# Whole-tile instructions for the middle tiles of a SiLU-and-multiply kernel

## The chip, the cores and the metric

The kernel runs on one core of one Trainium2 chip; the metric is device time in microseconds (us). "Span" in a profile is the time from its first to its last instruction, about 2 us less than the device time of the same run. ACT is the engine that evaluates functions (ScalarE), DVE the one that works on vectors (VectorE), SP the one that here issues stores (SyncE). Sixteen DMA engines move data between HBM and the on-chip memory. MB are 10^6 bytes; the profile's "4096.0 KB" is 4096 x 1024 bytes.

## The reference, cut to what matters

```python
x = np.random.randn(32, 512, 2048).astype(np.float32)   # 16384 rows of 2048

def reference(x):
    x1, x2 = x[..., :1024], x[..., 1024:]
    return (x1 * (1 / (1 + np.exp(-x1))) * x2).astype(np.float32)
```

134.22 MB are read and 67.11 MB written, each once. The arithmetic is one activation over half of the input and one multiply of the two halves.

## The kernel before

The rows are cut into 16 tiles. A tile has 128 partitions with K = 8 rows each: 8.39 MB in, 4.19 MB out. Input and output each have two buffers. Loads are issued from ACT's instruction stream, stores from SP's.

```python
K = 8
KC = 2
in_pool = ctx.enter_context(tc.tile_pool(name="in_pool", bufs=2))
out_pool = ctx.enter_context(tc.tile_pool(name="out_pool", bufs=2))
# ... load(i): nc.scalar.dma_start(out=xt..., in_=view(x_flat, i)) ...
load(0)
load(1)
for i in range(n_tiles):
    # ...
    for c in range(0, k, KC):               # 4 chunks of 2 rows
        ce = min(c + KC, k)
        nc.scalar.activation(out=ot[:, c:ce, :], in_=xt[:, c:ce, :half], func=Silu)   # shortened
        nc.vector.tensor_mul(out=ot[:, c:ce, :], in0=ot[:, c:ce, :], in1=xt[:, c:ce, half:])
        if last:
            nc.sync.dma_start(out=ov[:, c:ce, :], in_=ot[:, c:ce, :])
    if not last:
        nc.sync.dma_start(out=ov, in_=ot[:, :k, :])
    if i + 2 < n_tiles:
        load(i + 2)                          # waits for the tile's last multiply
```

With four chunks, DVE multiplies chunk 0 while ACT works on chunk 1: in the timeline below, ACT works from 73.53 to 80.84 us and DVE from 75.47. The schedule is kept as written: each engine does its instructions in this order, as when the next load's issue at 84.40 us follows the last multiply's end at 84.37.

## Time and profile before

| | before |
|---|---|
| device time | 470.82 us (470.62 to 471.04, 3 runs) |
| ACT busy, DVE busy | 25%, 30% of the span |
| DMA | 201.35 MB, 429 GB/s over the span |
| from one tile's start to the next | 29.03 us (mean of 14; the prediction takes 29.06) |

First, the totals by engine from the page of the kernel before: busy us, share of the span, instructions.

```profile
DVE 142.3 (30%) x64; ACT 118.2 (25%) x65; POOL 0.2 (0%) x4
```

Both compute engines are idle for more than two thirds of the time. The window table shows who is not. Its columns are the stretch and its length, busy us (and instructions) of DVE, ACT and POOL, the granted clock, the mean busy share of the DMA engines, and GB/s.

```profile
44.50:55.40 10.90, 8.89 (x4) 7.31 (x4) 0.00 (x0) 1.00 1.00 433
55.40:73.50 18.10, 0.00 (x0) 0.00 (x0) 0.00 (x0) 1.00 1.00 434
...
102.60:200.00 97.40, 35.20 (x16) 29.23 (x16) 0.00 (x0) 1.00 1.01 436
```

The DMA share is 1.00 whether the compute engines work (first line) or idle (second). The kernel is bound by DMA. Next, the timeline of two middle tiles: start, length, engine, source line, operation, and in brackets the idle time before it and what ended it.

```profile
73.53 7.31 ACT L87 ACTIVATE ot<-xt 128x2048 f32<-128x2048 f32 x4 [21.68 <-DMA xt<-in_x_dram]
75.47 8.90 DVE L92 TENSOR_TENSOR ot<-ot,xt 128x2048 f32<-128x2048 f32 x4 [20.09 <-ACT ot L87]
84.40 0.37 ACTq L74 DMA_DIRECT2D xt<-in_x_dram  x1
102.62 7.31 ACT L87 ACTIVATE ot<-xt 128x2048 f32<-128x2048 f32 x4 [21.78 <-DMA xt<-in_x_dram]
```

A tile starts at 73.53 and the next at about 102.6. Compute takes 10.9 us, then both engines wait 18 us more for data. Last, the chain of waits that ended last (start, length, what), and the DMA issues with the median time from issue to landing.

```profile
55.41 47.19 DMA xt<-in_x_dram
...
102.62 1.92 ACT ot L87
...
104.57 8.91 DVE ot L92 x4
```

```profile
out_dram<-ot SPq DMA_DIRECT2D x15, 4096.0 KB, 39.8
xt<-in_x_dram ACTq DMA_DIRECT2D x16, 47.1
```

The tiles arrive every 29 us, so a load waits 18 us of its 47 behind the load before it (issued at 55.41 us, with the load before it landing at about 73.5).

### The profile page before, as it was taken

To read this page: it belongs to the slowest core of one execution; us is meant where nothing else is said; L and a number is where in the kernel's file an instruction comes from. 1 tells how busy PE (TensorE), PEld (TensorE's weight loads), DVE (VectorE), ACT (ScalarE), POOL (GpSimd) and SP (SyncE) were. 2 spreads that over 40 slices of the span, in tenths; PEclk is the share of its full clock that TensorE was granted. 3 is DMA by queue.
4 is the path that set the end of the run, shared out by engine and by line. 5 is a ranking of instruction groups with operands and counts; after the bars stand their busy time and mean duration, and the time that the engine had idled before them with its cause. 6 is when DMAs were issued, how large, how long until landed. Compare 5 with 4: busy or idle time off the path is not lost.

```text
span 468.9 us, 269 instructions
## 1 busy us (share of the span) xinstructions
DVE 142.3 (30%) x64; ACT 118.2 (25%) x65; POOL 0.2 (0%) x4
## 2 busy tenths in 40 slices
DVE  0070705106061160601507025070250702407034
ACT  1142406023060330603206032060420604106051
POOL 0000000000000000000000000000000000000000
DMA  9899999999999998999999999999999989999998
GB/s 431 375 447 403 447 447 447 403 419 431 447 447 403 447 492 363 442 492 391 458 403 439 456 447 403 409 442 447 447 403 444 467 386 447 442 419 481 400 409 354
DMA packets 5042, 201.35 MB, mean 429 GB/s; under 512 B 560, under 2 KB 560, under 8 KB 560
## 3 DMA queue, kind: packets, MB, share of 16 engines
q10 hardware_dynamic: 2304, 134.22, 66.4%
q1 hardware_dynamic: 2736, 67.11, 33.2%
q14 instruction: 2, 0.02, 0.0%
HBM read 134.22 MB, written 67.11 MB: 429 GB/s over the span
## 4 chain that ended last, share of the span: by engine, by line
DMA 80%; DVE 15%; ACT 3%; DVEq 0%; issue 0%
DMA xt<-in_x_dram 80%; DVE ot L92 15%; ACT ot L87 3%; DVEq L128 0%
## 5 line engine op out<-in xcount | busy, mean ns | idle before, releaser
L92 DVE TENSOR_TENSOR ot<-ot,xt 128x2048 f32<-128x2048 f32 x64 | 142.3, 2286 | 319.5 <-ACT ot L87 319.5
L87 ACT ACTIVATE ot<-xt 128x2048 f32<-128x2048 f32 x64 | 116.9, 1897 | 338.8 <-DMA xt<-in_x_dram 338.8
L87 ACT ACT_TABLE_LOAD x1 | 1.3, 1283 | 1.3 <-PEq L117 1.3
L117 POOL MEMSET const-uint8-127<- 128x1 uint8 x1 | 0.1, 102 | 0.0
L117 POOL MEMSET const-bfloat16-1.0<- 128x1 bf16 x1 | 0.1, 101 | 0.0
L117 POOL MEMSET const-float32-0.0<- 128x1 f32 x1 | 0.1, 98 | 0.2 <-issue 0.2
L117 POOL MEMSET const-float32-1.0<- 128x1 f32 x1 | 0.1, 98 | 0.0
## 6 DMA issues: line engine op xcount, KB each, us to landing
out_dram<-ot SPq DMA_DIRECT2D x15, 4096.0 KB, 39.8
out_dram<-ot SPq DMA_DIRECT2D x4, 1024.0 KB, 5.7
xt<-in_x_dram ACTq DMA_DIRECT2D x16, 47.1
```

Source lines behind the costliest of these rows:

```text
L87: nc.scalar.activation(out=ot[:, c:ce, :], in_=xt[:, c:ce, :half], func=mybir.ActivationFunctionType.Silu,)
L92: nc.vector.tensor_mul(out=ot[:, c:ce, :], in0=ot[:, c:ce, :], in1=xt[:, c:ce, half:],)
L117: nc = _bacc.Bacc("TRN2", target_bir_lowering=False, num_devices=1)
```

## The change

The intent is fewer, longer instructions. Tiles 1 to 14 take one activation and one multiply over all 8 rows, without the overhead of three further instructions on each engine. The first tile keeps its chunks so that the pipeline starts early, the last so that its stores can start early. The price is that within a middle tile DVE can no longer start before ACT has done the whole tile.

```diff
-    KC = 2
+    KC_EDGE = 2
...
-        for c in range(0, k, KC):
-            ce = min(c + KC, k)
+        kc = KC_EDGE if i in (0, n_tiles - 1) else k
+        for c in range(0, k, kc):
+            ce = c + kc
```

## The prediction

> **What bounds the kernel now.** The DMA engines. The page's slices show DMA at 9 tenths nearly throughout; the window table gives a DMA share of about 1.00 and 431 to 436 GB/s in every stretch from 44.5 to 451 us. 201.35 MB at 433 GB/s is 465 us of the 468.9 us span. DVE is busy for 30%, ACT for 25%. [...]
>
> The chain of waits alternates a load of 47.1 us, one ACT op of 1.92 us and four DVE ops of 8.91 us, for every second tile. But 47.1 us is no transfer time: tiles start 29.06 us apart (73.5 and 102.6 in the timeline), so 18 us of it is queueing behind the previous load. Each tile has 8 load packets of 64 KB and 8 store packets of 32 KB per DMA engine (from the page's queue counts); taken in turn, 96 KB at 433/16 GB/s is 3.63 us, and eight rounds are 29.05 us: the measured period.
>
> **What the change does to compute.** On tiles 1 to 14, ACT and DVE no longer overlap. One ACT op is 1893 ns, four take 7.31 us. [...] One DVE op takes 2284 ns, four take 8.90 us; 8192 elements should take about 8.7 us (estimate). Load end to last multiply grows from 10.87 us to about 15.75 us, so store i and load i+2 are issued 4.9 us later; the first at about 60.3 us instead of 55.4. Saved are three op overheads per tile and engine, worthless on engines idle two thirds of the time. Bytes, packets, first and last tile stay.
>
> **How much is on the critical path.** Read literally, the chain says seven changed tiles times 4.9 us: 34 us slower. I expect none of it. Load i+2 comes 15.75 us after load i landed, while load i+1 keeps the load queue filled until 29.06 us: 13 us of slack. Store i-1 lands 21.7 us after load i (11.0 + 39.8 - 29.06), so the store queue is still filled when store i comes, with some 6 us left. Tile i's activation needs store i-2 landed, 7.4 us before load i. If the store queue ran dry for a packet, loads would take the turn and bytes only change order. The tail is the same tile in the same chunks.
>
> **Predicted:** 470.8 us, 8 times in 10 between 469.6 and 472.2. Faster by over 2%: 0.01; within 2%: 0.96; slower by over 2%: 0.03.
>
> **What the profile should show.** ACT ops of 7.0 and DVE ops of 8.7 us on the middle tiles; ACT busy about 114.6 us, DVE about 140; tile starts still 29.06 us apart, the last at 451.0; issue to landing of loads down from 47.1 to about 42.2 us, of stores from 39.8 to about 34.9; the chain's DMA share down from 80% to about 72%, ACT up from 3% to 11%; DMA share still 1.00.
>
> **What would make it wrong.** [...] If store buffers come free too late, ACT would wait for a store. If an 8192-element op over eight strided rows cost more per element, the 13 us would shrink.

The forecast of 470.8 us is the time before, with none of the chain's 34 us added. The 34 us are seven times 4.9, and the sum behind the 4.9 us came to 15.75 us from load end to last multiply, against 10.87: about 7.0 us for the activation, 8.7 us for the multiply, and small gaps. The activation's term measured 7.03 us. The 8.7 us is the estimate beside the 8.90 us of four chunks; it measured 8.69 us.

## The result, and the profile after

| | before | after |
|---|---|---|
| device time, same rounds (6 runs each) | 470.94 us | 470.88 us |
| range | 470.62 to 471.61 | 470.64 to 471.60 |
| load landed to last multiply done, middle tile | 10.9 us | 15.8 us |
| load, issue to landing | 47.1 us | 42.2 us |
| store, issue to landing | 39.8 us | 34.8 us |

The ratio is 1.0 with a 95% interval of 0.9987 to 1.0013. Here and below, ratios are the mean time of one kernel's fast runs over that of the other's of the same rounds, so not quite the ratio of the quoted medians. The profiled run of the changed kernel was its slowest (471.6 us, span 469.5 us); that of before took 470.65 us. The 0.6 us between the spans is within the runs' scatter and says nothing about the change.

The totals by engine after:

```profile
DVE 139.5 (30%) x22; ACT 114.3 (24%) x23; POOL 0.2 (0%) x4
```

The groups of instructions by shape after (line, engine, operation, shapes, count, busy us, mean ns, idle before):

```profile
L93 DVE TENSOR_TENSOR ot<-ot,xt 128x8192 f32<-128x8192 f32 x14 | 121.7, 8692 | 283.8 <-ACT ot L88 283.8
L88 ACT ACTIVATE ot<-xt 128x8192 f32<-128x8192 f32 x14 | 98.4, 7029 | 301.9 <-DMA xt<-in_x_dram 301.9
```

ACT saved 3.9 us and DVE 2.8 us of busy time, on engines that were waiting anyway. The windows after:

```profile
44.50:60.30 15.80, 7.97 (x1) 7.03 (x1) 0.00 (x0) 1.00 1.07 462
60.30:73.50 13.20, 0.72 (x1) 0.00 (x0) 0.00 (x0) 1.00 0.92 400
...
102.60:200.00 97.40, 28.74 (x4) 28.12 (x4) 0.00 (x0) 1.00 1.00 434
```

A packet is counted where it starts, so short windows scatter (the first two); the long one shows a share of 1.00 and 434 GB/s, as before. The timeline after:

```profile
74.18 7.03 ACT L88 ACTIVATE ot<-xt 128x8192 f32<-128x8192 f32 x1 [21.89 <-DMA xt<-in_x_dram]
81.24 8.69 DVE L93 TENSOR_TENSOR ot<-ot,xt 128x8192 f32<-128x8192 f32 x1 [20.23 <-ACT ot L88]
89.97 0.37 ACTq L74 DMA_DIRECT2D xt<-in_x_dram  x1
103.21 7.03 ACT L88 ACTIVATE ot<-xt 128x8192 f32<-128x8192 f32 x1 [22.00 <-DMA xt<-in_x_dram]
```

The next load is issued 15.8 us after the tile's start instead of 10.9, and the next tile still starts 29.03 us after this one. The chain and the issues after:

```profile
61.05 42.13 DMA xt<-in_x_dram
...
103.21 7.04 ACT ot L88
...
110.27 8.70 DVE ot L93
```

```profile
out_dram<-ot SPq DMA_DIRECT2D x15, 4096.0 KB, 34.8
xt<-in_x_dram ACTq DMA_DIRECT2D x16, 42.2
```

Compute on the chain grew by 4.9 us per pair of tiles, and the load's time from issue to landing shrank by as much. The load did not get faster: it was queued later, behind the same work.

### The profile page after: what moved, and what is told of

Same layout as the page of the kernel before. It is cut to its first block, busy times and chain, and to the rows that moved or that the text cites. A ratio compares the mean times of both kernels' runs of the same rounds, so it can differ in the third digit from the quotient of the medians.

```text
span 469.5 us, 185 instructions
## 1 busy us (share of the span) xinstructions
DVE 139.5 (30%) x22; ACT 114.3 (24%) x23; POOL 0.2 (0%) x4
## 4 chain that ended last, share of the span: by engine, by line
DMA 72%; DVE 14%; ACT 11%; DVEq 0%; issue 0%
DMA xt<-in_x_dram 72%; DVE ot L93 14%; ACT ot L88 11%; DVEq L129 0%
## 5 line engine op out<-in xcount | busy, mean ns | idle before, releaser
L93 DVE TENSOR_TENSOR ot<-ot,xt 128x8192 f32<-128x8192 f32 (+1 forms) x22 | 139.5, 6362 | 322.9 <-ACT ot L88 322.9
L88 ACT ACTIVATE ot<-xt 128x8192 f32<-128x8192 f32 (+1 forms) x22 | 113.0, 5163 | 343.3 <-DMA xt<-in_x_dram 343.3
## 6 DMA issues: line engine op xcount, KB each, us to landing
out_dram<-ot SPq DMA_DIRECT2D x15, 4096.0 KB, 34.8
xt<-in_x_dram ACTq DMA_DIRECT2D x16, 42.2
```

## The experiments

All twelve runs gave correct results. Two theories of why the time stood still, and rivals:

- **Slack.** The DMA queues hold enough work that later issues are absorbed. The cost is zero until the queues run dry, and shows in full where nothing is queued.
- **Cancelling.** The saved overhead repays the lost overlap.
- **Utilisation.** Longer compute costs nothing as long as no engine comes near 100% busy.

### serial_chunks: lose the overlap, save no instruction

Middle tiles do four activations, then four multiplies:

```diff
+        if not edge:
+            for c in range(0, k, KC):
+                nc.scalar.activation(out=ot[:, c:c + KC, :], ...)
+        for c in range(0, k, KC) if edge else range(k - KC, -1, -KC):
             ...tensor_mul of chunk c...
```

> The kernel before with, on tiles 1 to 14, all four activations of 2 rows first and then the four multiplies (in reverse order, so that the first waits for the last activation): the overlap is lost, no op is saved. Load end to last multiply about 16.2 us (7.31 + 8.90) against 10.87. Theory of slack (the DMA queues hold work for some 13 us of loads and 6 us of stores more): same, 470.9 us within 0.3%. Rival, two effects that cancel (fewer op overheads gain what the lost overlap costs): here only the loss is left, so slower; at most 14 x 5.3 = 74 us, clearly over 2%.

Measured: 470.83 us (5 runs) against 470.86 us, ratio 1.0001 (0.9989 to 1.0014). The timeline shows that the edit did what it should: the multiplies start only when the fourth activation is done, and the next tile still starts 29.1 us after this one.

```profile
73.97 7.31 ACT L88 ACTIVATE ot<-xt 128x2048 f32<-128x2048 f32 x4 [21.53 <-DMA xt<-in_x_dram]
81.31 8.90 DVE L101 TENSOR_TENSOR ot<-ot,xt 128x2048 f32<-128x2048 f32 x4 [19.94 <-ACT ot L88]
...
103.05 7.31 ACT L88 ACTIVATE ot<-xt 128x2048 f32<-128x2048 f32 x4 [21.77 <-DMA xt<-in_x_dram]
```

The loss of overlap alone, with no saving beside it, costs nothing. The cancelling theory falls.

### one_buf_chunks and one_buf_whole: take the slack away

Both kernels with one input buffer; nothing is queued behind a load.

```diff
-    in_pool = ctx.enter_context(tc.tile_pool(name="in_pool", bufs=2))
+    in_pool = ctx.enter_context(tc.tile_pool(name="in_pool", bufs=1))
...
-    load(1)
...
-        if i + 2 < n_tiles:
-            load(i + 2)
+        if i + 1 < n_tiles:
+            load(i + 1)
```

> The kernel before with one input buffer instead of two: load i+1 is issued after the last multiply of tile i, so nothing is queued behind a load. Theory of slack: the tile period is compute 10.9 us plus a load beside a store, 29.06 us[...]: 42.4 us, about 676 us in all (665 to 690).

> The changed kernel with one input buffer. Theory of slack: with no load queued ahead, the whole 4.9 us of each middle tile appears: 47.3 us a tile, 14 x 4.9 = 68 us more than one_buf_chunks, about 745 us. Rival (longer ops cost nothing because ACT and DVE are mostly idle, or gain and loss cancel): equal to one_buf_chunks within 1%.

Measured: 687.16 us and 755.04 us (4 runs each, fast). The same change now costs 67.9 us, where 14 tiles times 4.87 us make 68.2. The author's sum had 31.5 us for a load beside a store. The levels are 11 and 10 us above the expectation, for the most part because such a load took 32.1 us from issue to landing. The chain of one_buf_whole:

```profile
81.08 32.21 DMA xt<-in_x_dram
...
113.38 7.04 ACT ot L87
...
120.44 8.70 DVE ot L92
...
129.16 32.04 DMA xt<-in_x_dram
```

Compare the 42 us of the changed kernel: 32 us is a load that starts beside a store on empty queues, and the other 10 us was queueing. (There a load stood 13.1 us behind the load before it, from 61.05 to 74.18 us, and landed 29.0 us later. The 3.1 us by which 32.1 us exceeds that did not show.) With the queue gone, longer compute shows in full. This supports slack and contradicts both rivals: ACT and DVE are even less busy here.

### act_x2, act_x3, act_x4: use the slack up

The changed kernel, with the whole-tile activation repeated on middle tiles (the result stays right, the repeats are waste on purpose):

```diff
-            nc.scalar.activation(...)
+            for _ in range(1 if kc == KC_EDGE else 2):      # 3 and 4 in the others
+                nc.scalar.activation(...)
```

> The changed kernel with the whole-tile activation issued twice on tiles 1 to 14 (same result): load end to multiply end about 22.7 us instead of 15.75. That is past the landing of the store before (about 21.7 us after the load), so the store queue runs empty for a packet or so, but short of 29.06 us, where the load queue would. Theory of slack: loads take the free turn, bytes only change order, 470.9 us within 0.3%; the last load lands about 2 us earlier (about 449) and more store is left after it. Rival, the store slack of 6 us is what counts: about 1 us a tile, 14 us slower. Rival of utilisation (only an engine near 100% costs time): same.

> As act_x2 with three activations: load end to multiply end about 29.7 us. Theory of slack as a loop over the two input buffers: compute plus the load's own time (29.06 us beside stores[...]) must stay under 2 x 29.06 us, so the knee is near 26.6 us, and this is 3 us past it; queue model made of this trace's packet times: 494 us (485 to 500), DMA share below 1.00. Rival of utilisation: ACT is busy 21 us of each 29.06, DVE 8.7, so the same, 471 us.

> Four activations: about 36.6 us from load end to multiply end. Theory of the two-buffer loop: about 543 us (530 to 555), that is about half of each extra 7 us a tile, as two buffers share it. Rival of utilisation: ACT is busy 28.0 us of each 29.06, still under 100%, so 471 us, or a few us more.

Measured (fast runs; before 470.86 us in the same rounds):

| | load landed to multiply done | device time | ratio |
|---|---|---|---|
| act_x2 | 22.8 us | 470.59 us (5 runs) | 0.9995 (0.9982 to 1.0009) |
| act_x3 | 29.9 us | 502.25 us (4 runs) | 1.067 |
| act_x4 | 36.9 us | 592.94 us (4 runs) | 1.2596 |

A middle tile of act_x2:

```profile
100.59 14.09 ACT L89 ACTIVATE ot<-xt 128x8192 f32<-128x8192 f32 x2 [15.06 <-DMA xt<-in_x_dram]
...
123.44 0.37 ACTq L74 DMA_DIRECT2D xt<-in_x_dram  x1
129.55 14.09 ACT L89 ACTIVATE ot<-xt 128x8192 f32<-128x8192 f32 x2 [14.86 <-DMA xt<-in_x_dram]
```

act_x2 more than doubles the compute time of the kernel before, at no cost. Its last load landed at 448.70 us in place of 451.58 (the changed kernel): where stores came late, loads took the turn, and more store bytes were left for the end (its four last stores took 8.0 us to land, 5.8 in the changed kernel, medians). By the packet records the store queue ran empty once (the second store was issued at 67.88 us, and the first one's last packet had ended at 63.80); from then on all stores came later and overlapped again. So the six microseconds of store slack that the prediction counted are not what counts. act_x3 is past the knee, with ACT busy 21 us of every 31: the utilisation theory falls. (This run alone would leave a rival: activation and multiply one after the other take 30.4 us here, from 75.04 to 105.42, which is itself over 29.03 us. act_x2_r3 below is slower too, and there they take 26.4 us.) act_x3 is some 8 us above its expectation, as a fresh load took 32.2 us (the chain repeats every 62.2 us: 29.9 of compute and that load), and as more stores are left at the end (its four last took 8.7 us to land). The author's sum had 31.6 us for a fresh load, and so the knee at 26.6 us; the 543 us for act_x4, from the same loop, rest on it too.

act_x4 was 50 us slower than the slack theory gave. Its timeline shows why:

```profile
82.04 0.37 ACTq L74 DMA_DIRECT2D xt<-in_x_dram  x1
82.51 28.21 ACT L89 ACTIVATE ot<-xt 128x8192 f32<-128x8192 f32 x4 [9.23 <-DVE ot L94]
110.76 8.69 DVE L94 TENSOR_TENSOR ot<-ot,xt 128x8192 f32<-128x8192 f32 x1 [28.75 <-ACT ot L89]
119.48 0.37 ACTq L74 DMA_DIRECT2D xt<-in_x_dram  x1
119.95 28.21 ACT L89 ACTIVATE ot<-xt 128x8192 f32<-128x8192 f32 x4 [9.22 <-DVE ot L94]
```

ACT sits idle for 9.2 us while DVE multiplies, then issues the load, then starts the next tile. The load stands in ACT's own instruction stream and has to wait for the multiply, so a tile costs ACT plus DVE: 37.44 us from 82.51 to 119.95.

### act_x4_sp and after_sp: is it ACT's own load issue?

```diff
-        nc.scalar.dma_start(out=xt[:, :plan[i][1], :], in_=view(x_flat, i))
+        nc.sync.dma_start(out=xt[:, :plan[i][1], :], in_=view(x_flat, i))
```

> act_x4 with the loads issued from SP instead of ACT. act_x4 took 593 us where the two-buffer loop alone gave 543; its trace shows ACT idle for 9.2 us a tile until the multiply ended. Theory: ACT is held by its own load issue, which waits for the multiply of the same tile, so a tile costs ACT plus DVE, 37.4 us; with the issue on SP, ACT goes on and the two-buffer loop is left: (36.9 + 32.1)/2 = 34.5 us a tile, about 545 us (535 to 560). Rival, ACT waits for the multiply for another reason (for instance the output buffer): 593 us again.

> The changed kernel with the loads issued from SP, as control for act_x4_sp: loads and stores now go through one queue in order. All theories: same, 470.9 us within 0.5%, as one full queue keeps the DMA engines as busy as two.

Measured: act_x4_sp 544.71 us (4 runs) against 592.94 us of act_x4, as expected. With the issue on SP, ACT starts the next tile while DVE still multiplies:

```profile
71.18 8.69 DVE L94 TENSOR_TENSOR ot<-ot,xt 128x8192 f32<-128x8192 f32 x1 [38.22 <-ACT ot L89]
72.09 28.21 ACT L89 ACTIVATE ot<-xt 128x8192 f32<-128x8192 f32 x4 [0.94 <-DMA xt<-in_x_dram]
```

The hold is ACT's own load issue, and in the kernels before and after it is harmless only because the multiply ends long before the next tile's data lands (before: 84.37 against 102.6 us; after: 89.93 against 103.2).

after_sp missed its expectation: 475.09 us (6 runs) against 470.99, ratio 1.0086 (1.0071 to 1.01). Here one queue in order was slightly worse than two in turn. In its window from 2 to 451 us the DMA share is 1.00 at 430 GB/s where the changed kernel has 431, and its last load lands about 1 us later; that is only part of the 4 us. In the packet records of its trace, 125 of the 2048 load packets took over 2.5 us, where 2.42 us is the median, against 34 in the changed kernel; that is 1.7 us more on each engine. Why is open.

### act_x2_r3 and act_x2_r6: where is the knee?

act_x2 with one more activation over the first 3, or 6, of the 8 rows:

```diff
+            if kc != KC_EDGE:
+                nc.scalar.activation(out=ot[:, :3, :], in_=xt[:, :3, :half], func=Silu)   # :6 in r6
             nc.vector.tensor_mul(...)
```

> act_x2 with a third activation over 3 of the 8 rows (3072 elements, about 2.65 us): load end to multiply end about 25.4 us. act_x3 and the one-buffer pair show a load landing 32.1 us after issue when nothing is queued before it. Two-buffer loop: (25.4 + 32.1)/2 = 28.8 us a tile, under the 29.06 us that the DMA engines need, so the same, 470.9 us within 0.5%. Theory of the prediction (load slack until 29.06 us): same too.

> The third activation over 6 of the 8 rows (about 5.2 us): about 28.0 us from load end to multiply end. Two-buffer loop: (28.0 + 32.1)/2 = 30.05 us a tile, 1.0 us over, times 14: about 485 us (481 to 488), DMA share about 0.97. Theory of the prediction (13 us of slack, knee at 29.06 us): still the same, 471 us. One ACT-then-DVE pass is 28.5 us here, so that limit does not bind.

Both expectations for act_x2_r3 failed: 482.84 us (482.18 to 487.29, 4 runs), ratio 1.0266 (1.023 to 1.0302). act_x2_r6 took 492.55, 500.24, 500.56 and 500.76 us. A run counts as slow here when it is over 1.5% above the kernel's fastest, so three of the four do; but no run was near 471 us, and none near 485. From the chain of act_x2_r3, its loads in order, one left out:

```profile
70.31 32.16 DMA xt<-in_x_dram
...
128.13 32.30 DMA xt<-in_x_dram
...
186.09 32.37 DMA xt<-in_x_dram
...
303.71 35.14 DMA xt<-in_x_dram
...
364.52 35.55 DMA xt<-in_x_dram
...
425.73 35.53 DMA xt<-in_x_dram
```

The first three are 58 us apart, two tiles at the full DMA rate, as the loop over two buffers had it (25.6 + 32.3 us). Then the loads take longer, up to 35.5 us, and two tiles take 60.8 to 61.2 us. The windows of act_x2_r3 show what changed:

```profile
74.00:232.00 158.00, 43.46 (x5) 94.66 (x17) 0.00 (x0) 1.00 0.99 428
306.00:423.00 117.00, 32.07 (x4) 67.28 (x12) 0.00 (x0) 1.00 1.00 414
```

The DMA engines stay fully busy but move less. In the packet records, 208 load packets took over 2.5 us, up to 4.4 us; since about 300 us there are 27 to 29 of them for each load, most 3 to 8 us after its issue, which add 1.1 to 1.4 us to each of the 16 engines. That is about what each tile is over 29.03 us: half of 60.8 to 61.2 us is 1.4 to 1.6 us more. In act_x3, a load's first packets start only after the load before has ended. There the store that is issued at the same time comes first: its first packets start 0.83 us after the issue and take about 1.9 us, where 1.21 us is the median. The load's first packets follow, 2.8 us after the issue, and take about 3.1 us, where 2.42 us is the median. That adds 0.7 us for the load and 0.7 us for the store to each engine and tile. The load that opens the kernel before, on empty queues and without a store, shows it too: its first 16 packets took 3.1 us (median). So starting transfers on queues that have run dry cost DMA time in these runs, by these records. Why it sets in only after some tiles of act_x2_r3 is open.

The knee thus lies between 22.8 us (act_x2, free) and 25.6 us (act_x2_r3, 2.7%).

### last_whole and first_whole: what the edge chunks are worth

```diff
-        kc = KC_EDGE if i in (0, n_tiles - 1) else k
+        kc = KC_EDGE if i == 0 else k                 # last_whole
+        kc = KC_EDGE if i == n_tiles - 1 else k       # first_whole
```

> The changed kernel with the last tile whole too (one activation, one multiply, one store); only the first keeps chunks. After the last load lands at about 451 us nothing is queued but the store before; the last store starts 15.8 us later and moves 4.19 MB, 9.7 us. Theory: slower by about 10.8 us (7 to 13), about 481.7; the tail is the one place where lost overlap is paid. Rival (chunks don't matter anywhere): same.

> The changed kernel with the first tile whole too; only the last keeps chunks. The first store is issued 4.9 us later, at about 37.9 us, but load 1 is queued until 44.5 us. Theory of slack: same, 470.9 us within 0.3%, so the exemption of the first tile buys nothing. Rival: 4.9 us slower, as the pipeline fills later.

Measured: last_whole 481.05 us (4 runs) against 471.21 us, ratio 1.021 (1.0196 to 1.0224). A window of last_whole after its last load:

```profile
458.00:467.70 9.70, 8.69 (x1) 0.91 (x1) 0.00 (x0) 1.00 0.00 0
```

The same window of the changed kernel:

```profile
458.00:467.70 9.70, 4.42 (x3) 0.89 (x1) 0.00 (x0) 1.00 0.95 399
```

The DMA engines stand still for 9.7 us while the last tile is computed. Here nothing is queued, and overlap is worth its full price: 9.8 us of device time.

first_whole: 471.55 us (5 runs) against 471.21 us, ratio 1.0003 (0.9989 to 1.0017). Chunks in the first tile buy nothing. Its waits look entirely different, though:

```profile
ACT ot L88 <- DMA out_dram<-ot: 309.3, 14, 23.1
ACT ot L88 <- DMA xt<-in_x_dram: 31.8, 2, 19.5
```

ACT waits for 14 stores to free output buffers instead of for loads, with no change in time. Here DMA is the bound either way (429 GB/s over the span in both), and which transfer ACT waits for last changed with their order alone.

No run beat both kernels, and at the 434 GB/s of the middle windows little room is left: 201.35 MB take 464 us of a span of 469. Whether a kernel could move more was not tried.

## Why the prediction was right

- **The bound.** Predicted: DMA, at a ceiling. Measured: a DMA share of 1.00 and 434 GB/s in the changed kernel's window from 102.6 to 200 us (436 in the kernel before). That this rate is a ceiling was the assumption; the profiles show only that none of the windows of 97 us or more that were asked for had over 439 GB/s.
- **The mechanism.** Predicted: 4.9 us later issues, absorbed by queued work, though the chain read literally said 34 us. Measured: the chain's load time fell from 47.1 to 42.2 us as its compute rose. one_buf_whole shows that the same 4.9 us costs 68 us without the queue, and serial_chunks that nothing cancels.
- **The sizes.** Predicted 7.0 and 8.7 us for the long instructions, ACT 114.6 us and DVE about 140 us busy, issue to landing 42.2 and 34.9 us, 72% and 11% of the chain for DMA and ACT; measured 7.03 and 8.69 us, 114.3 and 139.5 us, 42.2 and 34.8 us, 72% and 11%.
- **The 13 us of load slack were too many.** They assumed that a load may be issued as late as the moment when the load before it lands. Measured: 7.0 us are free (22.8 less 15.8, act_x2), 9.8 us are not (25.6 less 15.8, act_x2_r3). A load needed a lead: on an empty queue it took 32.1 us, and tiles come every 29.03 us. That alone would put the limit at 26.0 us (2 x 29.03 less 32.1, an estimate); act_x2_r3 at 25.6 us was slower already, and part of that stays open. The change used 4.9 us, so the conclusion stood.
- **The 6 us of store slack were no limit.** act_x2 went past them, its store queue ran empty once, and the time stayed at 470.59 us; as the prediction said, bytes only changed order.
- **Not foreseen:** ACT's own load issue makes a tile cost ACT plus DVE. At 15.8 us a tile it does not bind; in act_x4 it cost 48 us.

## What to carry to other kernels

Before costing a change from the chain of waits, ask which part of a transfer's time from issue to landing is queueing: compare it with the period at which transfers arrive. In these runs compute added before an issue was free until the queue would run dry, and the limit lay between 22.8 and 25.6 us, some microseconds before the moment at which the previous load lands (29 us). Overlap was worth its price where nothing was queued: in the last tile (9.8 us) and not in the first (0.3 us, within the scatter).

## What else the traces show

- **Shares of the two queues.** What these traces record as a packet is 64 KB (loads) or 32 KB (stores), one for each partition's contiguous rows. In the kernel before, the packets start by turns from 60 to 90 us, 16 of the loads and 16 of the stores (one turn of each is double). From 60 to 440 us the load packets' time is 66.2% of the 16 engines', the store packets' 33.6%, with 109.05 and 55.05 MB moved. In one_buf_whole, where load and store packets alternate too, a load of 8.39 MB and a store of 4.19 MB, issued together, landed after 32.1 and 31.9 us (medians). Other packet lengths were not tried side by side.
- **Starting on empty queues.** In act_x3 and one_buf_whole, a load and a store issued together on empty queues had their first packet, the store's, 0.83 us after the issue started; the issue itself takes 0.33 us. The load's first packet came after the store's, 2.7 to 2.8 us after the issue, and the first packets of both took 0.7 us longer than their medians of 2.42 and 1.21 us.
- **Issues and engines.** An issue that waited held back the issuing engine's later work: 592.94 us with loads issued from ACT, 544.71 us from SP (act_x4, act_x4_sp). And two queues were slightly better than one in order: 475.09 us for after_sp, 470.99 us for the kernel before in the same rounds.
- **Length of an activation.** 1893 ns for 2048 elements in a partition, 7029 ns for 8192. From these two, an estimate: 0.836 ns an element and 181 ns an instruction. It gives 2749 ns for the 3072 elements of act_x2_r3, where 2.76 us were measured.
